# Dealing projection steps beside attention and mLSTM heads with a carried balance, and three more of them at the first head

## The chip, the cores and the metric

The kernel runs on one core of a Trainium2 chip. The metric is the time of one execution on the device in microseconds (us); the tables give a median over runs, and the profile shows one of these executions instruction by instruction. PE is TensorE (the matrix engine, PEld its weight loads), DVE is VectorE, ACT is ScalarE, POOL is GpSimd, SP issues most of the transfers.

## The reference

One layer of a hybrid decoder: 512 tokens, model width 2048, float32. Both branches read the same normed input through one projection `w_in`; their gated sums go through `w_out`.

```python
h = rms_norm(x, norm_g)
q_a, k_a, v_a, o_a, i_a, f_a, z_a, c_q, c_kv, k_r, z_b, g_a, g_b = split(h @ w_in)
# branch A: 8 mLSTM heads (qk 128, v 256)
q_a, k_a = split(silu(causal_depthwise_conv(concat(q_a, k_a), conv_w)))   # 4 taps
h_a = rms_norm(mlstm_chunkwise(q_a, k_a, v_a, i_a + b_i, f_a + b_f), mlstm_norm_g)
y_a = (sigmoid(o_a) * h_a * silu(z_a)) @ w_a
# branch B: latent attention, 16 heads (128 + 64 rotary)
q_b = rms_norm(rms_norm(c_q, q_lat_g) @ w_uq)      # then rope on the last 64
k_b, v_b = rms_norm(c_kv, kv_lat_g) @ w_ukv        # k_b normed with k_r, then rope
o_b = causal_softmax_attention(q_b, k_b, v_b)
y_b = (o_b * silu(z_b)) @ w_b
out = x + (sigmoid(g_a) * y_a + sigmoid(g_b) * y_b) @ w_out
```

## The kernel before

Every large product is made of three matmuls of a high and a low part of each operand (`mm3`, L113): ACT casts the high part, DVE subtracts for the low part (`split`, L104 to 107; its instructions show as L105 and L106). Weights stream in tiles through the SP queue and are split as they are used (`load_w`, L142). A projection is a generator that issues one step of its inner dimension at a time and yields how many columns PE was given: 6144 for a token-wise step with 512 columns (`proj_tok`, L169), 4608 with 384, 3072 for a channel-wise step of two blocks (`proj_ch`, L183).

The order of the work is written out by hand, and the framework then sorts each engine's queue by its own estimate of when an instruction can run. The parts are:

1. Latents, norm and the products of most of `w_in` in a seven-product (Strassen) form, to about 1040 us. Gates, values and the like go to DRAM and are read again later.
2. Latent transposes (two generators, four requests of 2000 each) beside the first of eight q/k blocks of `w_in` (`block_qk`, 16 steps of 3072); then the first pair projection; the mLSTM gates (requests of 6000, 3000 and 4000) beside the second block.
3. Attention in eight pairs of heads (`pair_attn`, L931). Each pair makes 11 requests for filler, the first of 8000 (`KEYS_AHEAD`), ten of 7800 (`ATTN_STEP`). In a request S is scores and softmax, X the transposes of the probabilities, O the product with the values. Beside pairs 0 to 6 the filler is the rest of a begun q/k block, then the projection of the next pair (`pair_proj`: four steps of 4608, four of 6144; behind it POOL takes a reciprocal root and scales the keys, L809 to 829), then further q/k blocks. What is left of a begun block and of the projection is drained at the end of each pair (L1076). Beside pair 7 the filler is the first seven steps of the `w_b` projection (`out_b`, L1044), a cap set by memory that opens only after attention.
4. mLSTM heads (`heads`, L1229): eight heads with eight requests each (`MLSTM_STEP`): four for the decay-weighted products j (`wda`, `wdb`, `sta`, `stb`), four for the sums i with the values (`num`). Within the same requests the convolution of the next head (`head_conv`), its loads (`head_load`) and the scaling and transposing of the previous head (`head_scale`, `head_out`) are issued. After the last head four requests (`OUT_AHEAD`) stand around its scaling. The filler is the rest of `w_b`, 64 steps of 6144 in all. Ahead of the heads the convolution and loads of head 0 are issued in turn with filler steps (L1251 to 1255).
5. What is left of `w_b` (L1259), then `w_a` and `w_out`. `w_a` reads the gated heads back from DRAM (`reload`, L1017; `ga_d`), at most six tiles ahead.

Requests meet filler in `weave` (L201): for each request it takes steps until the columns asked for are reached. A step can't be divided, and what a step gives beyond the request is forgotten with the next one.

Of the kernel before, what the change touches and what calls it, by code (L numbers as in the profile page):

```python
# [36 lines left out]
NB_RAW, NB_W, NB_L, NB_A, NB_B, NB_HEAD, NB_T, NB_ACC, NB_AUX = 4, 3, 2, 15, 12, 17, 6, 5, 3  # L37
NB_X, NB_RING, NB_HI, NB_LO = 5, 8, 3, 2

KEYS_AHEAD, ATTN_STEP, MLSTM_STEP, OUT_AHEAD, G_AHEAD = 8000, 7800, 4500, 8000, 6  # L40
EARLY = {"lat", "c", "gz", "vh", "vl", "rope", "rk"}


# [1 line left out]
def hybrid_kernel(  # L45
# [151 lines left out]
    def drain(gen):  # L197
        for _ in gen:
            pass

    def weave(main, filler):  # L201
        for want in main:
            while want > 0:
                got = next(filler, None)
                if got is None:
                    break
                want -= got


    sap = open_pool("sap")  # L210
# [833 lines left out]
    def out_b(d):  # L1044
        def evac(t, ps):
            u = u_t[d]
            V.scalar_tensor_tensor(u[:, t, :], u[:, t, :], 1.0, ps, ALU.add, ALU.mult)

        for k, want in enumerate(proj_tok(load_w(w_b, d * 512, 512, KD), 512, get_gb, KD, evac)):
            if k == H8:  # L1050
                u_t.append(pools["up"][1].tile([P, T, 512], F32, tag=f"u{d}", name=f"u{d}"))
                SP.dma_start(u_t[d], gb_g[d])
            yield want

    cs = [dict() for _ in range(8)]
    blocks = [block_qk(n) for n in range(8)]
    weave(chain(*lats), blocks[0])
    drain(blocks[0])
    drain(pair_proj(0, cs[0]))
    weave(mlstm_gates(), blocks[1])  # L1060
    drain(blocks[1])
    del blocks[:2]
# [9 lines left out]
    for p in range(7):  # L1072
        proj = pair_proj(p + 1, cs[p + 1])
        first = chain(ahead(True), proj)
        weave(pair_attn(p, cs[p]), chain(first, ahead()))
        drain(first)  # L1076
        cs[p] = None
# [8 lines left out]
    filler = chain(*(out_b(d) for d in range(4)))  # L1086
# [7 lines left out]
    def head_conv(h, c):  # L1094

        xs, parts = [], []
        for n in range(2):
            xp = tmp(516, "xp")
            G.memset(xp[:, 0:3], 0.0)
            SP.dma_start(xp[:, 3:515], qk_d[h][:, n, :])  # L1100
            xs.append(xp)

        def conv(n):
            xp, k = xs[n], 8 * n + h
            o = big([P, 2, S], F32R, "qkT")
            c["kT" if n else "qT"] = o
            b = tmp(512, "cv")

            def taps(j0, j1):
                for j in range(j0, j1):  # L1110
                    V.scalar_tensor_tensor(b, xp[:, j:j + S], cw[:, k, j:j + 1], b, ALU.mult, ALU.add)

            with behind_weights():
                V.tensor_scalar(b, xp[:, 3:515], cw[:, k, 3:4], None, ALU.mult)
                taps(0, 1)
            yield
            taps(1, 3)
            th = xp[:, 0:512]
            A.activation(th, b, AF.Tanh, scale=0.5)
            yield  # L1120
            V.scalar_tensor_tensor(b, th, 1.0, b, ALU.add, ALU.mult)
            A.copy(o[:, 0, :], b)
            yield
            V.tensor_tensor(o[:, 1, :], b, f32(o[:, 0, :]), ALU.subtract)
            yield

        q, k = conv(0), conv(1)
        for turn in ((), (), (), (q,), (q, k), (q, k), (q, k), (k,)):
            for part in turn:
                next(part)  # L1130
            yield
# [97 lines left out]
    def heads():  # L1229
        for h in range(H_A):  # L1230
            conv = ahead = iter(())
            if h + 1 < H_A:
                conv, ahead = head_conv(h + 1, hs[h + 1]), head_load(h + 1, hs[h + 1])
            for n, want in enumerate(head_mlstm(h, hs[h])):
                next(conv, None)
                next(ahead, None)
                if h and n == 4:
                    head_scale(h - 1, hs[h - 1])
                if h and n == 6:
                    head_out(h - 1, hs[h - 1])  # L1240
                yield want
            drain(conv)
            drain(ahead)
        for _ in range(2):
            yield OUT_AHEAD
        head_scale(H_A - 1, hs[H_A - 1])
        for _ in range(2):
            yield OUT_AHEAD
        head_out(H_A - 1, hs[H_A - 1])

    start = head_conv(0, hs[0])  # L1251
    for load in head_load(0, hs[0]):
        next(start)
        next(filler)
    drain(start)
    weave(heads(), filler)
    close_pool("bph")
    g2p = open_pool("g2p")
# [82 lines left out]
```

## Time and profile before

| | us |
|---|---|
| median of 3 runs | 2158.21 (2154.21 to 3683.05) |
| profiled execution, its own time | 2155.99 |
| its span, first to last instruction | 2154.3 |
| PE busy in it | 2101.4 (98%) |
| DVE busy | 1461.9 (68%) |
| ACT busy | 1007.7 (47%) |
| POOL busy | 167.4 (8%) |

A profile row gives what an engine did and, in brackets, how long it stood idle before it and what released it. PEclk is the clock that TensorE was granted, as a share of 2.4 GHz; it has two levels, 1.2 and 2.4 GHz, so a value between 0.5 and 1 is a mixture over the stretch. Matmuls are pipelined, so one that lasts 0.39 us on its row can be followed by the next after 0.23 us.

### The profile page before, as it was taken

To read this page: it belongs to the slowest core of one execution; us is meant where nothing else is said; L and a number is where in the kernel's file an instruction comes from. 1 tells how busy PE (TensorE), PEld (TensorE's weight loads), DVE (VectorE), ACT (ScalarE), POOL (GpSimd) and SP (SyncE) were. 2 spreads that over 40 slices of the span, in tenths; PEclk is the share of its full clock that TensorE was granted. 3 is DMA by queue.
4 is the path that set the end of the run, shared out by engine and by line. 5 is a ranking of instruction groups with operands and counts; after the bars stand their busy time and mean duration, and the time that the engine had idled before them with its cause. 6 is when DMAs were issued, how large, how long until landed. Compare 5 with 4: busy or idle time off the path is not lost. (4 is left out here: it accounts for less than half of the span.)

```text
span 2154.3 us, 30176 instructions
## 1 busy us (share of the span) xinstructions
PE 2101.4 (98%) x10776; PEld 1803.1 (84%) x10776; DVE 1461.9 (68%) x2304; ACT 1007.7 (47%) x2025; POOL 167.4 (8%) x306
## 2 busy tenths in 40 slices
PE   8999999999999999999999999989999978999999
PEld 8888888888888999988888888877778866888889
DVE  6888888887778778788556566568787764443233
ACT  8544455444444444444454455466455553222221
POOL 0000100000000000000022222033111110000000
PEclk9999999999999999999999999999999988999999
DMA  6655535633652452462733333432475536332443
GB/s 171 169 178 176 172 114 193 220 114 97 186 152 88 152 176 79 138 205 86 261 103 102 99 102 103 120 94 84 137 245 191 182 133 199 109 136 93 135 130 118
DMA packets 210183, 309.17 MB, mean 144 GB/s; under 512 B 31984, under 2 KB 99952, under 8 KB 209008
## 3 DMA queue, kind: packets, MB, share of 16 engines
q1 hardware_dynamic: 187248, 271.58, 41.0%
q10 hardware_dynamic: 22784, 35.66, 4.7%
q8 instruction: 84, 1.38, 0.3%
q14 instruction: 67, 0.55, 0.1%
HBM read 252.66 MB, written 54.53 MB: 143 GB/s over the span
## 5 line engine op out<-in xcount | busy, mean ns | idle before, releaser
L106 DVE TENSOR_TENSOR wlo<-raw,whi 128x512 fp32r<-128x512 f32 (+3 forms) x368 | 243.4, 663 | 327.1 <-PE acc L115 232.9
L105 ACT CAST whi<-raw 128x512 fp32r<-128x512 f32 (+3 forms) x368 | 218.9, 596 | 445.9 <-PE acc L116 322.7
L106 DVE TENSOR_TENSOR wl<-rx,wh 128x1024 fp32r<-128x1024 f32 x192 | 234.9, 1224 | 131.5 <-PE aux L535 58.8
L105 ACT CAST wh<-rx 128x1024 fp32r<-128x1024 f32 x192 | 202.4, 1055 | 211.3 <-PE acc L536 97.2
L105 ACT CAST wh<-rr 128x1024 fp32r<-128x1024 f32 x144 | 151.7, 1053 | 200.6 <-PE aux L536 91.7
L114 PE MATMUL acc<-whi,g 128*128 128x512 f32 x512 | 199.3, 397 | 8.1 <-ACT g L105 6.8
L115 PE MATMUL acc<-wlo,g 128*128 128x512 f32 x512 | 202.2, 395 | 0.3 <-DVE wlo L106 0.3
L116 PE MATMUL acc<-whi,g 128*128 128x512 f32 x512 | 201.9, 394 | 0.0
L106 DVE TENSOR_TENSOR wl<-rr,wh 128x1024 fp32r<-128x1024 f32 x144 | 175.7, 1220 | 31.5 <-PE aux L535 13.9
L535 PE MATMUL acc<-wl,sh 128*128 128x512 f32 x400 | 155.6, 389 | 0.0
L536 PE MATMUL acc<-wh,sl 128*128 128x512 f32 x400 | 155.6, 389 | 0.0
L534 PE MATMUL acc<-wh,sh 128*128 128x512 f32 x400 | 155.4, 389 | 0.0
L114 PEld LDWEIGHTS acc<-whi,g 128*128 128x128 f32 x512 | 96.3, 190 | 26.7 <-ACT g L105 7.2
L483 DVE TENSOR_TENSOR rx<-rr,rx 128x1024 f32<-128x1024 f32 x96 | 116.9, 1222 | 2.2
L115 PEld LDWEIGHTS acc<-wlo,g 128*128 128x128 f32 x512 | 97.3, 190 | 20.7 <-DVE wlo L106 2.0
L116 PEld LDWEIGHTS acc<-whi,g 128*128 128x128 f32 x512 | 97.1, 190 | 20.3 <-DVE g L106 0.2
L114 PE MATMUL acc<-whi,y 128*128 128x512 f32 (+1 forms) x320 | 111.1, 348 | 0.0
L116 PE MATMUL acc<-whi,y 128*128 128x512 f32 (+1 forms) x320 | 111.0, 347 | 0.0
L115 PE MATMUL acc<-wlo,y 128*128 128x512 f32 (+1 forms) x320 | 111.0, 347 | 0.0
L114 PE MATMUL acc<-whi,lat 128*128 128x384 f32 (+1 forms) x256 | 94.9, 373 | 0.8 <-ACT junk L792 0.5
L115 PE MATMUL acc<-wlo,lat 128*128 128x384 f32 (+1 forms) x256 | 93.5, 365 | 0.0
L534 PE MATMUL aux<-wh,sh 128*128 128x512 f32 x240 | 93.4, 389 | 0.0
(389 smaller groups left out, 5293.4 us busy)
## 6 DMA issues: line engine op xcount, KB each, us to landing
rr<-in_w_in SPq DMA_DIRECT2D x144, 512.0 KB, 4.6
rx<-in_w_in SPq DMA_DIRECT2D x48, 512.0 KB, 5.0
raw<-in_w_in SPq DMA_DIRECT2D x64, 256.0 KB, 2.8
raw<-in_w_b SPq DMA_DIRECT2D x64, 256.0 KB, 3.6
raw<-in_w_a SPq DMA_DIRECT2D x64, 256.0 KB, 3.1
raw<-in_w_out SPq DMA_DIRECT2D x64, 256.0 KB, 3.0
raw<-in_w_ukv SPq DMA_DIRECT2D x32, 256.0 KB, 2.9
raw<-in_w_uq SPq DMA_DIRECT2D x32, 192.0 KB, 2.4
```

The source lines that it names most:

```text
L105: hi = A.copy(dst_hi, src)
L106: lo = V.tensor_tensor(dst_lo, src, f32(dst_hi), ALU.subtract)
L114: PE.matmul(ps, lh, rh, start=start, stop=False)
L115: PE.matmul(ps, lh, rl, start=False, stop=False)
L116: PE.matmul(ps, ll, rh, start=False, stop=stop)
L483: V.tensor_tensor(dst, a, b, ALU.subtract)
L534: PE.matmul(out[i], lh[:, tok], hi[:, n, :], start=first, stop=False, skip_group_check=cont)
L535: PE.matmul(out[i], lh[:, tok], lo[:, n, :], start=False, stop=False, skip_group_check=cont)
L536: PE.matmul(out[i], ll[:, tok], hi[:, n, :], start=False, stop=k == H8 - 1, skip_group_check=cont)
```

## The change

`weave` carries a balance: each request is added to it, steps are taken while it is positive, and their columns come off it, so that a surplus counts against the next request. The balance starts at zero in each call. When the filler is used up, the rest of the main work is drained. Two constants are smaller, `MLSTM_STEP` 3900 instead of 4500 and `OUT_AHEAD` 6000 instead of 8000. At the first head, where the remaining two parts of its convolution were drained without filler, three turns issue one part (if any is left) and one filler step each.

```diff
--- before.py
+++ after.py
@@ -37,7 +37,7 @@
 NB_RAW, NB_W, NB_L, NB_A, NB_B, NB_HEAD, NB_T, NB_ACC, NB_AUX = 4, 3, 2, 15, 12, 17, 6, 5, 3
 NB_X, NB_RING, NB_HI, NB_LO = 5, 8, 3, 2
 
-KEYS_AHEAD, ATTN_STEP, MLSTM_STEP, OUT_AHEAD, G_AHEAD = 8000, 7800, 4500, 8000, 6
+KEYS_AHEAD, ATTN_STEP, MLSTM_STEP, OUT_AHEAD, G_AHEAD = 8000, 7800, 3900, 6000, 6
 EARLY = {"lat", "c", "gz", "vh", "vl", "rope", "rk"}
 
 
@@ -199,12 +199,15 @@
             pass
 
     def weave(main, filler):
+
+        balance = 0
         for want in main:
-            while want > 0:
+            balance += want
+            while balance > 0:
                 got = next(filler, None)
                 if got is None:
-                    break
-                want -= got
+                    return drain(main)
+                balance -= got
 
 
     sap = open_pool("sap")
@@ -1252,7 +1255,9 @@
     for load in head_load(0, hs[0]):
         next(start)
         next(filler)
-    drain(start)
+    for _ in range(3):
+        next(start, None)
+        next(filler)
     weave(heads(), filler)
     close_pool("bph")
     g2p = open_pool("g2p")
```

## Rows read from the trace of the kernel before

**Rows 1.** The first line of the page, the profiled execution

```profile
span 2154.3 us, 30176 instructions
```

**Rows 2.** Windows: stretch, length; busy PE, PEld, DVE, ACT, POOL; clock, DMA share, GB/s

```profile
150.00:200.00 50.00, 50.00 (x223) 41.39 (x222) 38.63 (x45) 23.35 (x26) 0.00 (x0) 1.00 0.68 201
...
1350.00:1400.00 50.00, 50.00 (x264) 42.99 (x263) 28.41 (x66) 23.09 (x51) 2.83 (x6) 1.00 0.42 125
1400.00:1450.00 50.00, 42.81 (x219) 36.45 (x218) 33.88 (x88) 32.85 (x108) 14.26 (x17) 0.93 0.31 95
1450.00:1500.00 50.00, 46.56 (x255) 38.85 (x254) 41.18 (x108) 32.91 (x113) 16.49 (x21) 1.00 0.27 87
1500.00:1550.00 50.00, 46.98 (x252) 38.22 (x252) 38.24 (x102) 25.94 (x66) 12.51 (x18) 1.00 0.23 80
1550.00:1600.00 50.00, 47.08 (x215) 38.22 (x214) 36.22 (x68) 22.78 (x56) 5.27 (x25) 0.97 0.84 284
...
1650.00:1700.00 50.00, 50.00 (x257) 42.55 (x255) 38.42 (x83) 27.30 (x73) 7.82 (x29) 1.00 0.58 190
...
1750.00:1800.00 50.00, 28.52 (x132) 23.73 (x131) 29.64 (x67) 25.41 (x65) 5.58 (x16) 0.73 0.44 147
1800.00:1850.00 50.00, 50.00 (x230) 41.31 (x229) 21.78 (x33) 14.66 (x25) 0.00 (x0) 1.00 0.48 159
```

**Rows 3.** Timeline of POOL and PE at pair 5: start, length, instruction, [idle before, releaser]

```profile
1423.78 2.93 POOL L121 TENSOR_TENSOR rs_y<-ms,mhalf 128x16 f32<-128x16 f32 x1 [11.38 <-DVE ms L811]
...
1431.26 1.11 PE L867 MATMUL aux<-ident,kn 128*128 128x128 f32 x4 [5.41 <-POOL kn L829]
```

**Rows 4.** Timeline of PE around the end of pair 6

```profile
1497.87 0.48 PE L114 MATMUL acc<-whi,g 128*128 128x512 f32 x1
...
1513.96 0.60 PE L867 MATMUL aux<-ident,qn 128*128 128x128 f32 x4
```

**Rows 5.** Timeline of PE in the heads: heads 2 and 6 begin, one filler step

```profile
1624.14 0.39 PE L1158 MATMUL aux<-nT,pick 128*128 128x512 f32 x1
...
1736.31 0.40 PE L114 MATMUL acc<-whi,g 128*128 128x512 f32 x1
...
1739.04 0.39 PE L1158 MATMUL aux<-nT,pick 128*128 128x512 f32 x1
```

**Rows 6.** Timeline of PE at the end of the heads, three longest waits

```profile
1759.82 0.80 PE L114 MATMUL aux<-qkT,qkT 128*128 128x512 f32 x1 [3.93 <-ACT qkT L1122]
...
1780.65 1.94 PE L1221 MATMUL aux<-ident,og 128*128 128x128 f32 x8 [4.84 <-DVE og L1215]
...
1789.36 0.79 PE L114 MATMUL acc<-whi,g 128*128 128x512 f32 x1 [6.77 <-ACT g L105]
```

**Rows 7.** Windows of 5 us with a granted clock below 1.00, columns as in rows 2

```profile
1430.00:1435.00 5.00, 3.74 (x16) 3.74 (x17) 1.71 (x3) 1.85 (x3) 2.48 (x4) 0.50 0.00 0
...
1580.00:1585.00 5.00, 5.00 (x19) 4.02 (x19) 5.00 (x10) 3.71 (x11) 0.00 (x0) 0.80 0.91 312
...
1760.00:1765.00 5.00, 2.53 (x7) 1.69 (x7) 2.31 (x8) 1.25 (x5) 2.21 (x7) 0.50 0.25 86
1765.00:1770.00 5.00, 2.88 (x10) 2.29 (x11) 4.29 (x11) 3.13 (x9) 1.31 (x3) 0.50 0.00 0
1770.00:1775.00 5.00, 5.00 (x31) 4.80 (x30) 0.58 (x2) 3.40 (x12) 0.07 (x1) 0.69 0.00 0
...
1790.00:1795.00 5.00, 5.00 (x16) 3.96 (x15) 4.24 (x8) 3.71 (x7) 0.00 (x0) 0.64 1.01 378
```

**Rows 8.** Timeline of DVE in head 1, head 2 and the last head

```profile
1619.99 0.69 DVE L106 TENSOR_TENSOR wlo<-raw,whi 128x512 fp32r<-128x512 f32 x1 [3.82 <-issue]
...
1626.37 0.69 DVE L1183 SCALAR_TENSOR_TENSOR wda<-aux,wda 128x512 f32<-128x512 f32 x1 [1.30 <-POOL vl L1141]
...
1763.75 0.48 DVE L1215 SCALAR_TENSOR_TENSOR og<-num,rsn,og 128x256 f32<-128x256 f32 x1 [2.65 <-POOL rsn L1208]
```

**Rows 9.** Timeline of the SP queue, transfers of the gated heads

```profile
1784.13 7.64 SPq L1023 DMA_DIRECT2D g<-ga  x13
```

## The prediction, made before the result was known

> **What bounds the kernel now.** I read the page first: the span [rows 1] and, in the 40 slices, a TensorE (PE) busy almost everywhere except in the slices around 1430 and around 1780 us. Then the table of windows of 50 us [rows 2]: the 25 windows from 150 to 1400 us (first and last shown) are a full 50.00 of PE, and so is the first one after 1800 us, where the two last projections begin. What PE idles behind its start-up lies in two places: 7.19 + 3.44 + 3.02 + 2.92 = 16.6 us in 1400 to 1600 (the last attention pairs and the first mLSTM head) and 21.5 us in 1750 to 1800 (the last heads). So PE's work is the bound, and this change neither adds nor removes a matmul. It can win only what PE waits, and what runs slowly because PE has waited.
>
> The second part is read from windows of 5 us [rows 7]. Where PE had just waited, the granted clock is 0.50, the lower of its two levels (1.2 against 2.4 GHz), or a mixture. The time lost is busy time times (1 - clock): 3.74 x 0.5 = 1.9 us at 1430, 5.00 x 0.2 = 1.0 at 1580, 1.3 + 1.4 + 1.6 at 1760 to 1775, 1.8 at 1790; together 9.0. Idle and slow time make a pool of 16.6 + 21.5 + 9.0 = 47.1 us. If all of it went, the span would be 2107.2.
>
> **Why PE waits there.** Every step of attention or a head asks for filler columns, and a `weave` without a balance rounds each request up to whole steps and forgets the surplus. I counted the steps by hand from the code.
>
> - Attention. 7800 columns are served as three q/k block steps (9216), or two projection steps (9216 to 12288). The six remaining blocks, 96 steps, are gone in the fourth request of pair 4; its last three requests and the last seven of pairs 5 and 6 get nothing. That leaves 13.7 us of idle time in 1400 to 1550 (16.6 less the 2.9 of the first head's window). The longest piece is a pair boundary [rows 3]: the reciprocal root on POOL begins at 1423.78, and PE's transposes of the scaled keys wait 5.41 us for POOL until 1431.26.
> - Heads. A request of 4500 is served by one whole step of 6144. 64 steps less 7 (pair 7) less 6 (head start) are 51, one for each request; they end with the third request of head 6. Five requests of head 6 and all eight of head 7 run bare, and nothing is left for the tail. The chain of PE's waits shows it [rows 6]: 3.93 us for the convolved q/k of head 7, 4.84 for the scaled output, 6.77 for the first reloaded gate rows, whose transfers were issued behind the last stores [rows 9].
>
> **The change, part by part.**
>
> 1. *Balance in attention.* The 11 requests of a pair are 86,000 columns; pair projection is 43,008 (4 x 4608 + 4 x 6144). With the surplus carried, a pair takes 28 block-sized steps instead of 33, so the blocks last into the fifth request of pair 6, and only its last request is empty. The gaps inside pairs 4, 5 and 6 should close. What stays: the balance is zeroed at each `weave`, and the projection now ends late. In pair 5 four block steps follow it, 24 matmuls of 2.73 / 12 = 0.228 us [rows 5], 5.5 us against the POOL chain of 1431.26 - 1423.78 = 7.5 [rows 3]: I take 1 us of wait with attention's own matmuls in between. In pair 6 no filler follows, so I put the whole old boundary there once more: 5.4 + 1.9 of slow clock. Pair 7 still has seven steps, now over five requests instead of four, as its cap is unchanged; the order of the queues already spreads them, as a w_b matmul at 1497.87, well ahead of pair 7's first transposes at 1513.96, shows [rows 4]. I leave it the 3.0 us of window 1500 to 1550. New waits: 1 + 7.3 + 3.0 = 11.3 us. Bounds: 0, if w_b steps are drawn into the boundary, and the 13.7 + 1.9 of now, if nothing closes.
>
> 2. *Three more steps at the first head.* They are 36 matmuls, 8.2 us at 2.73 a step [rows 5], with three weight loads, three splits on ACT and on DVE (0.69 us each on DVE [rows 8]), and splits of reloaded rows. They stand beside head 0's convolution, where PE waited 2.9 us and ran 1.0 us too slowly [rows 2, 7]. The splits come into DVE's queue ahead of head 0's own chain, where DVE is full (5.00 of 5 us at 1580 [rows 7]): about 2 us, under 8.2 us of PE. New wait 1 us; bounds 0 and 3.9.
>
> 3. *Balance in the heads, 3900 instead of 4500.* 48 steps are left. 64 requests of 3900 take 249,600 / 6144, rounded up 41; the four of 6000 at the end make it 45, and three are left for the drain. Head 0 gets 6, every other head 5, the tail 4 + 3. A head takes 28.73 us now, (1739.04 - 1624.14) / 4 from the first matmul of head 2 to that of head 6, eight steps of 2.73 in it [rows 5]. With five, PE needs 28.73 - 3 x 2.73 = 20.5 us. This is the doubtful step, as a head then has to fit DVE too. DVE is busy 38.42 of 50 us amid the heads, or 22.1 us in 28.73 [rows 2]; three splits less make 20.0. Its waits in the chain of a head come on top: 1.30 us for the exponentials and the causal selection before the first product [rows 8]; the 3.82 us wait there is slack and goes first. 20.0 + 1.3 = 21.3. The upper bound adds the 2.65 us that DVE stood behind POOL's reciprocal root in the bare head [rows 8]: 24.0. The lower is PE's 20.5. I take 22.0, in the middle, because a step now is either there or not (requests get 1, 0, 1 ...), so PE meets the bare chain three times a head: 1.5 us of idle time, 10 us over heads 1 to 7; bounds 0 and 7 x 3.5 = 24.
>
> 4. *Tail.* Two steps before the last scaling and two behind it, 10.9 us, cover the 4.84; the three drained, 8.2 us, cover the 6.77 [rows 5, 6]. The 13 gate transfers keep SP for 7.64 us [rows 9], and weight loads behind them may be late: 1 us; bounds 0 and 7.
>
> 5. The same `weave` beside the latents gives six steps instead of eight, beside the gates five as before; a drain follows each at once and PE is full there: nothing, as the same matmuls fill the same stretch. If they did not, it would cost at most the two steps that leave, 12 matmuls of 0.228 us or 2.7 us. `return drain(main)` does what the old `break` did.
>
> **Sum.** 2154.3 - 47.1 + 11.3 + 1 + 10 + 1 = 2130.5 us of span. The profiled run's time was 1.7 us above its span (2155.99), so 2132; the median of the shown runs, 2158.21, is 2.2 above the profiled run. That is 1.2% below the median, well inside the 2% (some 43 us) that a measurement of this kernel can tell from no change.
>
> **Rivals.**
>
> - *The clock sags.* Thin filler makes many short waits instead of a few long ones. For: at 1580 the clock averaged 0.80 [rows 7], though that window of 50 us held but 2.9 us of waits [rows 2]. Against: 1450 to 1550 has 6.5 us of short waits at 1.00 [rows 2]. With half of that sag, 0.90, over seven heads of 20.5 us: 144 x (1 / 0.9 - 1) = 16 us more, 2148. The Trainium skill ("TensorE: Matmul & The Clock Gate", section "A second HAM failure mode: psum-queue depth-cycling") says that frequent small idles between groups of matmuls make the clock go back and forth between its two levels; by that rule the heads would get slower exactly because filler is rationed. The trace agrees with it at 1580 and disagrees at 1450 to 1550, so it gets a small chance.
> - *The heads become a chain, and the kernel gets slower.* DVE takes its queue in order; if the scaling of the previous head is put ahead of a head's first product, as in the bare head at 1763.75 [rows 8], each head stands behind POOL's reciprocal root and the convolution behind that. Without the heads' idle time the gain is 47.1 - 13.3 = 33.8 us, or 4.8 us for each of seven heads: from a period of 25.3 us on, the kernel is slower than before. If the period stayed at 28.7, it would be 7 x 8.2 = 57 us of idle time, 2154.3 - 33.8 + 57 = 2178 of span, 2180. Against: DVE's 22.1 us contain no such wait now. Slower by 2% needs a period above 31.
> - *Dealing changes nothing.* The order on the queues is not the written one [rows 4]; if that order already moves filler to where it is needed, only names change: 2152 to 2160. Against: rows 6 show waits that no order could fill, since no step was left.
> - *Nearly all waits go.* No boundary stall and heads at PE's 20.5: 2109 to 2115.
>
> **How the numbers follow.** Forecast (2116 to 2146) 0.68; clock 0.10; heads slower than before 0.08; nothing 0.07; nearly all 0.07. The predicted time is the forecast's 2132. The range runs from 2112, half way into the last case, to 2151, past the clock case; that leaves out some 0.18. Faster by over 2% needs under 4 us of new waits in all: 0.05. Slower by over 2%: 0.02. Within 2%: 0.93.
>
> **What would show it.** Right: no window from 1440 to 1500 with more than 1 us idle; one wait of about 5 us for the scaled keys before pair 7 and none before pair 5; first matmuls of heads 20.5 to 23.5 us apart; nothing above 2 us between the last head and the first w_a matmul; a clock of 1.00 in the heads. Wrong: heads 25 us or more apart, with PE waiting for products or convolutions of DVE; a clock below 0.9 in several windows of the heads; w_a's first weights late.

## The result, and the profile after

| | before | changed |
|---|---|---|
| median, us | 2157.07 (4 runs) | 2136.43 (2135.75 to 2137.48, 4 runs) |
| ratio to the kernel before | | 0.9909, 95% interval 0.9890 to 0.9929 |
| span of the profiled execution | 2154.3 | 2135.0 |

The change saves 20 us, 0.9%; 2132 had been predicted, in a range of 2112 to 2151. The single outlying run of the kernel before (3683.05) is left out of the ratio.

Windows of 50 us of the changed kernel answer to [rows 2], with the same columns:

```profile
1350.00:1400.00 50.00, 49.36 (x266) 42.92 (x265) 34.70 (x84) 27.88 (x88) 14.19 (x18) 1.00 0.33 98
1400.00:1450.00 50.00, 45.94 (x237) 40.09 (x236) 28.83 (x74) 25.61 (x82) 12.76 (x14) 0.97 0.35 103
1450.00:1500.00 50.00, 47.16 (x238) 39.78 (x237) 36.77 (x87) 29.35 (x78) 6.52 (x8) 0.96 0.41 136
1500.00:1550.00 50.00, 44.28 (x228) 37.01 (x225) 31.95 (x84) 25.11 (x69) 10.03 (x16) 0.93 0.23 80
1550.00:1600.00 50.00, 47.97 (x226) 39.79 (x225) 39.17 (x72) 22.46 (x51) 3.33 (x15) 0.97 0.81 280
...
1650.00:1700.00 50.00, 47.63 (x254) 40.46 (x255) 44.57 (x97) 32.15 (x90) 10.65 (x33) 1.00 0.63 206
...
1750.00:1800.00 50.00, 48.14 (x217) 39.62 (x216) 26.42 (x42) 21.67 (x36) 1.39 (x6) 1.00 0.69 236
1800.00:1850.00 50.00, 50.00 (x230) 41.29 (x229) 19.23 (x29) 12.72 (x22) 0.00 (x0) 1.00 0.33 114
```

PE's idle time in 1750 to 1800 has gone from 21.5 us to 1.9. In its place every window of the heads has a little (2.4 us in 1650 to 1700, where there was none). But in 1400 to 1550 there are 4.1 + 2.8 + 5.7 = 12.6 us, where there were 13.7, and 0.6 in 1350 to 1400, where there was none: beside attention the idle time has only moved.

Where PE stands now is in its timeline (start, length, instruction, idle before it and releaser); the lines answer to [rows 3, 5, 6]:

```profile
1434.23 0.39 PE L116 MATMUL acc<-whi,lat 128*128 128x512 f32 x1
...
1447.19 1.11 PE L870 MATMUL aux<-ident,kn 128*128 128x128 f32 x4 [4.06 <-POOL kn L832]
...
1485.55 0.44 PE L910 MATMUL aux<-ident,pr 128*128 128x128 f32 x2 [1.26 <-DVE go L931]
...
1490.25 0.52 PE L910 MATMUL aux<-ident,pr 128*128 128x128 f32 x3 [1.31 <-ACT junk L795]
...
1515.21 1.12 PE L870 MATMUL aux<-ident,kn 128*128 128x128 f32 x4 [5.65 <-POOL kn L832]
...
1568.80 1.43 PE L114 MATMUL acc<-whi,g 128*128 128x512 f32 x4 [1.80 <-ACT whi L105]
...
1598.30 0.39 PE L1161 MATMUL aux<-nT,pick 128*128 128x512 f32 x1
...
1707.62 0.39 PE L1161 MATMUL aux<-nT,pick 128*128 128x512 f32 x1
...
1760.83 1.03 PE L1224 MATMUL aux<-ident,og 128*128 128x128 f32 x8
...
1771.90 0.50 PE L114 MATMUL acc<-whi,g 128*128 128x512 f32 x1 [1.86 <-ACT g L105]
```

Two pair boundaries wait for the scaled keys, 4.06 us ahead of pair 6 and 5.65 ahead of pair 7; before the change it was one of 5.41. In pair 6 there are two waits of 1.3 us, released by DVE's gated output (`go`) and by ACT's sums of squares (`junk`). The start of the first head waits 1.80 us. From the first matmul of head 1 (1598.30) to that of head 6 (1707.62) it is 21.9 us a head. The transposes of the last head at 1760.83 wait for nothing, and the first matmul of `w_a`, at 1771.90, waits 1.86 us instead of 6.77.

Windows of 5 us of the changed kernel, to be set beside [rows 7]:

```profile
1445.00:1450.00 5.00, 2.81 (x11) 2.61 (x12) 0.84 (x2) 1.27 (x2) 3.18 (x4) 0.67 0.14 45
...
1485.00:1490.00 5.00, 3.26 (x13) 2.11 (x13) 4.80 (x14) 4.77 (x15) 0.00 (x0) 1.00 0.65 220
1490.00:1495.00 5.00, 4.65 (x14) 3.63 (x15) 5.00 (x10) 4.60 (x20) 4.38 (x4) 0.66 0.38 113
...
1515.00:1520.00 5.00, 4.79 (x23) 4.43 (x24) 2.23 (x4) 3.17 (x6) 1.80 (x4) 0.66 0.01 2
...
1570.00:1575.00 5.00, 4.77 (x16) 3.67 (x16) 3.10 (x6) 2.88 (x7) 0.29 (x1) 0.70 0.68 247
```

The clock still falls behind four of these waits, to 0.66 to 0.70 as a mean of 5 us, but not behind the 1.86 us ahead of `w_a`; busy time times (1 - clock) is 0.9 + 1.6 + 1.6 + 1.4 us. In the heads it stays at 1.00.

The gain by place: the last stores of attention's outputs are issued 1.3 us later than before. The SP queue before and after:

```profile
1552.13 0.33 SPq L929 DMA_DIRECT2D gb<-go  x1
...
1553.44 0.32 SPq L932 DMA_DIRECT2D gb<-go  x1
```

From there to the first `w_a` matmul it is 1789.36 - 1771.90 + 1.3 = 18.8 us less, and the 1.8 us of slow clock behind it are gone [rows 6, 7]. So the heads bring all of the 19.3 us of span, and attention brings nothing.

### The profile page after: what moved, and what is told of

It is laid out like the page before. It is cut to its first block, busy times and chain, and to the rows that moved or that the text cites. A ratio compares the mean times of both kernels' runs of the same rounds, so it can differ in the third digit from the quotient of the medians.

```text
span 2135.0 us, 30145 instructions
## 1 busy us (share of the span) xinstructions
PE 2096.4 (98%) x10776; PEld 1801.6 (84%) x10776; DVE 1458.9 (68%) x2304; ACT 1005.9 (47%) x2025; POOL 173.0 (8%) x306
## 5 line engine op out<-in xcount | busy, mean ns | idle before, releaser
L116 PEld LDWEIGHTS acc<-whi,g 128*128 128x128 f32 x512 | 96.6, 189 | 20.1
L114 PE MATMUL acc<-whi,lat 128*128 128x384 f32 (+1 forms) x256 | 94.7, 372 | 0.2
L116 PE MATMUL acc<-whi,lat 128*128 128x384 f32 (+1 forms) x256 | 93.4, 365 | 0.0
```

The lines of the kernel that those rows point to most:

```text
L114: PE.matmul(ps, lh, rh, start=start, stop=False)
L116: PE.matmul(ps, ll, rh, start=False, stop=stop)
```

## Which place the gain comes from

First the balance beside attention alone, with the heads dealt as before:

```diff
     def weave(main, filler):          # with the balance, as changed
+    def weave_whole(main, filler):    # the old loop, whole steps
...
-    weave(heads(), filler)
+    weave_whole(heads(), filler)
-... MLSTM_STEP, OUT_AHEAD ... = ... 3900, 6000
+... MLSTM_STEP, OUT_AHEAD ... = ... 4500, 8000
-    for _ in range(3):                # three steps at the first head
-        next(start, None)
-        next(filler)
+    drain(start)
```

> The balance is kept beside the latents, gates and attention; the heads are dealt as before (whole steps, 4500 and 8000, no three extra steps). Theory: the whole gain is in the heads, and the balance only moves attention's waits from pairs 5 and 6 to two pair boundaries; in the changed kernel the last product of attention ended at 1552.5 us against 1551.2 before. Expected 2155 to 2160, no faster than before. Rival, the prediction's first term (the gaps of pairs 4 to 6 close, one boundary stays): 4 us less than before, about 2152. Rival, attention carries a good part of the 20 us: 2147 or less.

Measured: 2158.83 us, ratio 1.0005 (0.9995 to 1.0014). The balance beside attention alone brings nothing, neither the 4 us of the prediction nor more.

Then the other half:

```diff
-    weave(chain(*lats), blocks[0])
+    weave_whole(chain(*lats), blocks[0])       # and so beside gates and all pairs
     weave(heads(), filler)                     # balance, 3900, 6000 and three steps stay
```

> The balance works in the heads alone; attention is dealt as before, with 3900, 6000 and the three extra steps kept. Theory: 2133 to 2137, the same as the changed kernel or 1 to 3 us better, since the balance beside attention brought nothing. Rival, attention's balance is worth 4 us: 2140. Rival, worth much more: 2145 or above.

Measured: 2134.17 us, ratio 0.9889 (0.9875 to 0.9904), at least as good as the whole change. The gain is that of the heads, with their start and their tail.

What the balance beside attention costs shows at the first head. PE's longest wait there is 0.60 us in this kernel, at a clock of 1.00, against 1.80 us and 0.70 in the changed one; with the heads dealt as before the change, it is 2.74 us with the balance beside attention and 1.11 without:

```profile
1572.31 0.50 PE L115 MATMUL acc<-wlo,g 128*128 128x512 f32 x1 [0.60 <-DVE wlo L106]
```

## The three steps at the first head

```diff
-    for _ in range(3):
-        next(start, None)
-        next(filler)
+    drain(start)
```

> The changed kernel without the three steps at the first head: the end of head 0's convolution is drained bare, and six steps are left behind the heads instead of three. The prediction gave these steps 2.9 us (3.9 us of waits and slow clock less 1). In the changed kernel PE still waited 1.8 us there for the cast of a weight whose ACT queue stood behind the convolution, and the clock read 0.70 for 5 us, so some 3.5 us were not won. Theory: 2136 to 2138, 0 to 2 us worse than the changed kernel, as the steps come back in the drain. Rival: 2139 or more, if they really cover head 0's chain.

Measured: 2142.89 us, ratio 0.9929 (0.9914 to 0.9944), against 0.9909 and 0.9913 for the changed kernel: some 4 us worse, though the intervals overlap and the two did not run side by side. My expectation of 0 to 2 fell, and the rival, which was the prediction's own term, holds. Windows of 5 us of this kernel at the first head:

```profile
1570.00:1575.00 5.00, 2.65 (x11) 2.00 (x12) 4.79 (x10) 3.75 (x10) 0.51 (x1) 1.00 0.98 379
...
1580.00:1585.00 5.00, 3.67 (x24) 3.00 (x22) 4.81 (x12) 1.69 (x5) 0.61 (x3) 1.00 1.08 360
1585.00:1590.00 5.00, 3.85 (x11) 3.09 (x12) 5.00 (x8) 3.58 (x13) 0.00 (x0) 0.66 0.79 269
```

PE idles 2.4, 1.3 and 1.2 us in them and the clock falls, while DVE is 4.8 to 5.0 of 5 us busy. The longest wait is released by ACT, whose queue stands behind DVE's convolution of head 1:

```profile
1584.83 0.63 ACT L1122 ACTIVATE xp<-cv 128x512 f32<-128x512 f32 x1 [2.82 <-DVE cv L1114]
...
1586.15 0.58 PE L114 MATMUL aux<-vh,sta 128*128 128x258 f32 x1 [2.49 <-ACT junk L1199]
```

So head 0's products and head 1's convolution share DVE, and PE has too little to do beside them. The three steps cover most of that: PE's idle time in 1550 to 1600 is 5.0 us without them and 2.0 in the changed kernel, where the one long wait left is that of 1.80 us.

## What sets the pair boundary

POOL takes the reciprocal root of queries and keys together (16 columns: one power and four small steps), then scales the queries' root and the rotary keys, then the keys, for which PE waits. An experiment orders the keys first:

```diff
-        rsqrt(rs[all 16], ms[all 16], 16)
-        srq = ...; (rotary queries); krs = ...
-        G.tensor_tensor(kn, kn, rs[keys], ALU.mult)
+        rsqrt(rs[keys], ms[keys], 8)
+        G.tensor_tensor(kn, kn, rs[keys], ALU.mult)
+        rsqrt(rs[queries], ms[queries], 8)
+        srq = ...; (rotary queries); krs = ...
```

> The changed kernel with another order of POOL's work behind each pair projection: the reciprocal root of the keys alone (8 columns instead of 16) and the scaling of the keys come first, the queries' root and the rotary keys after. The chain that PE waits for at a pair boundary gets shorter by about 1.3 us for the root, 1.3 us for what stood before the scaling and, with 0.2 more, to some 4.5 us from 7.5. Theory (the two boundary waits of 4.1 and 5.7 us are this chain and nothing else): each shrinks by some 3 us, 2130 to 2133 in all. Rival, something else releases PE there (convolved or rotary operands, weights): the waits move to the next instruction, 2135 to 2137.

Measured: 2133.69 us, ratio 0.9891 (0.9875 to 0.9908). The waits are 3.2 and 5.1 us, shorter by 0.8 and 0.6 only. POOL's timeline ahead of pair 7 shows why:

```profile
1503.41 3.27 POOL L121 TENSOR_TENSOR rs_y<-ms,mhalf 128x8 f32<-128x8 f32 x2 [12.31 <-DVE ms L814]
...
1507.92 1.89 POOL L817 TENSOR_TENSOR kn<-kn,rs 128x1024 f32<-128x1024 f32 x1
```

Both roots (x2) stand ahead of the scaling: the framework's sort had put the queries' root up, so the chain from POOL's start to the scaled keys was 6.4 us instead of 7.4. The time is just above the theory's 2130 to 2133. The second version holds it back:

```diff
+        scaled = G.tensor_tensor(kn, kn, rs[keys], ALU.mult)
+        with tc.issue_after(scaled.ins):
+            rsqrt(rs[queries], ms[queries], 8)
```

> The changed kernel with the keys' root and scaling first on POOL, and the queries' root held in POOL's queue until the scaling is issued. The run before, without the hold, had both roots side by side ahead of the scaling: the chain from POOL's start to the keys' transposes fell only from 7.4 to 6.4 us, and each boundary wait by 0.6 to 0.8. Now the chain should be 1.7 (root of 8 columns) + 0.9 + 1.9 = 4.5 us. Theory (POOL's chain and nothing else): boundary waits of about 1 and 2.7 us instead of 4.1 and 5.7, 2128 to 2132. Rival (the next operand is late as well): waits move on, 2133 or more.

Measured: 2130.71 us, ratio 0.9886 (0.9871 to 0.9900). The timeline of PE at the two boundaries:

```profile
1441.88 0.66 PE L872 MATMUL aux<-ident,kn 128*128 128x128 f32 x4 [1.09 <-POOL kn L817]
...
1444.93 0.66 PE L858 MATMUL aux<-ident,krs 128*128 128x128 f32 x4 [1.26 <-POOL krs L834]
...
1507.26 0.90 PE L872 MATMUL aux<-ident,kn 128*128 128x128 f32 x4 [3.44 <-POOL kn L817]
```

The waits for the keys fall to 1.09 and 3.44 us, about as expected, and 1.26 us (0.85 at pair 7) come back behind them for the rotary keys, now behind the queries' root on POOL. So POOL's chain does release these waits. The shorter one is worth some 6 us beside the changed kernel on the same chip (2137.19 us, ratio 0.9913, next section); the 4 us of the first version rest on ratios whose intervals overlap, from kernels that did not run side by side.

But POOL's 7.4 to 7.8 us are only the second half of what has to be covered. In the changed kernel the last matmul of pair 6's projection is at 1434.23 and the keys' transposes run at 1447.19: 13 us. ACT and DVE first evacuate the projection, and POOL begins at 1439.4:

```profile
1439.39 2.93 POOL L121 TENSOR_TENSOR rs_y<-ms,mhalf 128x16 f32<-128x16 f32 x1 [12.20 <-DVE ms L814]
```

Attention's own matmuls fill some 2.7 us of the 13, so by this count seven or eight steps of 1.37 us have to lie behind the projection. The deal of the changed kernel has eight or more behind those of pairs 0 to 3, then six, four and none behind pairs 4 to 6, and the waits were 0, 0, 0, 0, 0.6, 4.1 and 5.7 us.

## A deal by whole blocks

Six blocks are left for seven pairs. This version puts one whole block behind each of the first six projections, and requests enough for both:

```diff
-        first = chain(ahead(True), proj)
-        weave(pair_attn(p, cs[p]), chain(first, ahead()))
+        first = chain(proj, blocks.pop(0) if blocks else ())
+        weave(pair_attn(p, cs[p]), first)
-... ATTN_STEP ... = ... 7800
+... ATTN_STEP ... = ... 8400
```

With it ran the changed kernel itself, for a comparison on one chip:

> The changed kernel once more, on the chip of this group, so that the other three can be compared with it and not only with the kernel before. Expected 0.991 of the kernel before, about 2137, with PE waiting 4.1 and 5.7 us for the scaled keys at the two last pair boundaries.

Measured: 2137.19 us, ratio 0.9913 (0.9896 to 0.9929), with the boundary waits that the first profile had (4.06 and 5.63 us). In pair 6 it differs: one wait above 1 us (1.32) instead of two, and the clock stays at 1.00. Its windows there:

```profile
1485.00:1490.00 5.00, 3.46 (x15) 2.08 (x14) 4.79 (x14) 5.00 (x18) 1.35 (x2) 1.00 0.84 259
1490.00:1495.00 5.00, 4.58 (x19) 3.11 (x17) 5.00 (x10) 4.59 (x18) 3.45 (x3) 1.00 0.05 20
```

> The changed kernel with another deal in attention: beside each of pairs 0 to 5 the next pair's projection comes first and exactly one whole q/k block (16 steps) behind it, with requests of 8400 (92,000 columns a pair against 92,160 of filler); pair 6 has the projection alone. Theory: a pair boundary waits for POOL when fewer than about six block steps lie behind the projection (in the changed kernel 6 steps gave 0.6 us of wait, 4 gave 4.1, none 5.7, eight and more none); with 16 steps there is no wait, and the bare pair 6 has its projection done long before its end. Attention's idle time falls from some 15 us to some 6 and its slow clock goes: 2124 to 2130. Rival: the bare pair costs as much as the boundaries did: 2134 or more.

Measured: 2118.28 us, ratio 0.9825 (0.9810 to 0.9840), 19 us less than the changed kernel beside it and better than the theory's 2124. Its windows of 50 us:

```profile
1350.00:1400.00 50.00, 50.00 (x257) 42.67 (x257) 31.73 (x81) 26.50 (x87) 13.07 (x15) 1.00 0.34 101
1400.00:1450.00 50.00, 50.00 (x261) 43.19 (x260) 34.37 (x88) 27.27 (x88) 14.59 (x18) 1.00 0.30 87
1450.00:1500.00 50.00, 48.02 (x260) 40.15 (x260) 41.01 (x101) 34.00 (x102) 14.58 (x18) 1.00 0.45 153
1500.00:1550.00 50.00, 48.08 (x243) 38.67 (x241) 37.89 (x89) 24.20 (x54) 2.23 (x11) 1.00 0.51 178
```

No pair boundary waits for POOL. Attention idles 2.0 us in 1400 to 1550, all of it in short waits, and 1.9 more belong to the first head; the clock is 1.00 throughout. The first head begins at 1546.5 us instead of 1565.6 in the changed kernel's run of this group. Of the 19.1 us between, 13.0 are idle time (6.0 against 19.1 us from 24 us to the first head), 3.5 are slow clock behind the long waits, and the remaining 2.6 were not taken apart.

At the first head the two waits of this kernel add up to more than the 1.80 and 0.23 us of the changed one, and the clock stays at 1.00:

```profile
1548.64 1.19 PE L114 MATMUL acc<-whi,g 128*128 128x512 f32 x4 [1.74 <-ACT whi L105]
1550.36 0.50 PE L115 MATMUL acc<-wlo,g 128*128 128x512 f32 x1 [0.53 <-DVE wlo L106]
```

Does that add up with the heads? The same deal with the heads of the kernel before:

```diff
-    weave(heads(), filler)
+    weave_whole(heads(), filler)     # 4500, 8000, drain(start), as before the change
```

> One whole q/k block behind each projection beside pairs 0 to 5 (requests of 8400, balance kept there), but the heads dealt as before the change: whole steps, 4500 and 8000, no three extra steps. It asks whether attention's and the heads' gains add up. Theory: attention's waits and the heads' lie in different stretches, so this deal is worth here what it was worth on the changed kernel (19 us): 2135 to 2140. Rival, what is won in attention is lost again where filler runs out in the heads: 2146 or more.

Measured: 2138.84 us, ratio 0.9906 (0.9888 to 0.9925). PE's waits at the end of its heads are those of [rows 6] to a hundredth:

```profile
1742.45 0.80 PE L114 MATMUL aux<-qkT,qkT 128*128 128x512 f32 x1 [3.93 <-ACT qkT L1133]
...
1763.11 1.30 PE L1232 MATMUL aux<-ident,og 128*128 128x128 f32 x5 [4.85 <-DVE og L1226]
...
1771.81 0.80 PE L114 MATMUL acc<-whi,g 128*128 128x512 f32 x1 [6.76 <-ACT g L105]
```

The two gains add up within the noise: 0.9906 x 0.9909 = 0.9816, where 0.9825 (0.9810 to 0.9840) was measured for both. Last, both cures of the boundary in one kernel:

> The two changes that gained on the changed kernel in one: one whole block behind each projection, and the keys' root and scaling first on POOL with the queries' root held behind them. Theory: they cure the same wait, and with 16 block steps behind the projection no wait for the scaled keys is left, so the second adds nothing: 2115 to 2120, as with the first alone. Rival, POOL's chain still costs something within the pairs: 2112 or less.

Measured: 2117.43 us, ratio 0.9803 (0.9788 to 0.9818). The interval just meets that of the deal alone, the spans of the two profiled executions stand the other way (2116.1 against 2113.2), and no wait for the scaled keys is left in either. Whether POOL's order adds anything there stays open.

## What limits a head

```diff
-... MLSTM_STEP ... = ... 3900
+... MLSTM_STEP ... = ... 3200
```

> The changed kernel with requests of 3200 instead of 3900 in the heads: four steps a head instead of five, ten left for the drain instead of three. It asks what else than PE limits a head. PE alone would need 28.73 - 3.9 x 2.73 = 18.1 us a head. Theory (DVE and the chain limit it): DVE needs 19.15 us a head in the changed kernel, 18.4 with one split less, and 1 to 2 us of waits on top: heads 20 to 21 us apart, PE idle 2 to 3 us in each instead of 0.7, 2144 to 2152. Rival (PE limits a head even so): heads 18 to 18.5 us apart, and the same total, 2135 to 2139.

Measured: 2145.20 us, ratio 0.9948 (0.9934 to 0.9963). From head 1 to head 6, and the stretch between:

```profile
1594.69 0.39 PE L1161 MATMUL aux<-nT,pick 128*128 128x512 f32 x1
...
1695.41 0.40 PE L1161 MATMUL aux<-nT,pick 128*128 128x512 f32 x1
```

```profile
1594.70:1695.40 100.70, 93.21 (x496) 78.39 (x495) 88.51 (x195) 65.59 (x178) 22.51 (x75) 0.98 0.64 208
```

A head takes 20.1 us in the mean of five, 2 more than the estimate from PE's matmuls. PE idles 1.5 us in each, less than the 2 to 3 expected, and its clock is 0.98; DVE is busy 17.7 us. In the changed kernel the same stretch (109.3 us) is

```profile
1598.30:1707.60 109.30, 105.15 (x556) 88.80 (x555) 93.17 (x203) 67.95 (x185) 25.49 (x76) 1.00 0.61 197
```

with 0.8 us of idle time a head and DVE busy 18.6 of 21.9 (the expectation had 19.15). So one step less takes 2.7 us of matmuls out of a head and shortens it by 1.7, and the kernel is 8 us slower. The longest waits with four steps are released by DVE, 1.24 us for `wda` and 1.88 for `wlo`:

```profile
1654.20 0.80 PE L115 MATMUL acc<-wlo,g 128*128 128x512 f32 x1 [1.88 <-DVE wlo L106]
```

Behind the latter the clock falls once, to 0.74:

```profile
1655.00:1660.00 5.00, 5.00 (x17) 3.99 (x17) 3.36 (x12) 2.65 (x8) 1.03 (x3) 0.74 0.39 132
```

What limits a head at four steps is thus PE's own work, 18.6 us of 20.1, plus waits for DVE's chain. Whether 20 us is a floor was not tried with still fewer steps.

The other way:

```diff
-... MLSTM_STEP ... = ... 3900
+... MLSTM_STEP ... = ... 4500
```

> The changed kernel with the old request of 4500 in the heads, balance kept: 47 of the 48 steps go into the heads (six each, five in the last), one stands in the tail and none is left for the drain. It asks what the smaller constant is for. Theory: heads 28.73 - 2.1 x 2.73 = 23 us apart with less PE idle time in each, but at the end the waits for the scaled output and for the first reloaded rows come back (4.8 and 6.8 us before, with one step of 2.7 us against them, and slow clock behind them): 2141 to 2148. Rival, the balance alone is what counts: 2135 to 2139.

Measured: 2148.23 us, ratio 0.9944 (0.9928 to 0.9959). At its end:

```profile
1771.59 1.82 PE L1224 MATMUL aux<-ident,og 128*128 128x128 f32 x8 [4.33 <-DVE og L1218]
...
1780.53 0.80 PE L114 MATMUL acc<-whi,g 128*128 128x512 f32 x1 [7.12 <-ACT g L105]
```

The two waits of the tail are back, 4.33 and 7.12 us, since only one step is left to lie in them; heads 1 to 5 begin 24.2 us apart. So 3900 is no detail: with the old request the rest of the change brings 12 of the 20 us.

## Why the prediction was right, and where it was not

- *The bound and the pool.* PE's idle and slow time, 47.1 us in two places, was the right frame: nearly all that these kernels won came out of it. The shortest span, 2113.2, is 6 us above the floor of 2107.2. The pool was 2 us too small: the windows of 5 us at 1575 (0.86), at 1425 (0.84) and from 1780 to 1790 (0.50) had a slow clock too and were not added.
- *Heads.* Predicted were 22.0 us a head, 10 us of idle time over seven of them and 1 us in the tail. Measured: 21.9 us, some 5 us over the seven (0.8 us a head from head 1 to head 6), 1.9 us in the tail. The path was right: PE is the bound and DVE with its waits comes close behind. That 22.0 and 21.9 agree so well is partly luck, as the terms behind it were off both ways: PE was taken at 20.5 us a head and is busy 21.0, its idle time at 1.5 and is 0.8, DVE at 20.0 and is busy 18.6. The rival in which each head stands behind POOL's root and the convolution did not come: DVE was busy in 18.6 of 21.9 us.
- *First head.* 2.9 us were predicted for the three steps; without them the kernel is some 4 us slower. The step holds, though 2.0 us of idle time and 1.4 of slow clock stayed where I had left 1.
- *Attention.* This step failed. I gave it 4.3 us (15.6 of now against 11.3 of new waits); it brought nothing. The mis-sized term is the boundary ahead of pair 6: 1 us predicted, 4.06 and 0.9 of slow clock measured. I had set four block steps against POOL's 7.5 us [rows 3], from the start of POOL's root, and left out the five us in which ACT and DVE evacuate the projection; from its last matmul it is 13 us. Ahead of pair 7, where the old boundary was put whole, 5.4 + 1.9 became 5.65 + 1.6, while the 3.0 us left for the short waits of 1500 to 1550 nearly vanished: the boundary accounts for all but 0.1 of that window's idle time. The first sign of being right also failed, since 2.2 us are idle in 1445 to 1450 and 1.7 in 1485 to 1490.
- *A wait not foreseen.* In pair 6, PE waits 1.26 and 1.31 us and then runs at 0.66. The second execution of the same kernel has a single wait above 1 us there and no slow clock, though nearly as much idle time in 1450 to 1500 (2.7 us against 2.8). In the first, ACT is busy 4.77 and DVE 4.80 of 5 us. Of the casts of the reloaded value outputs for `w_b`, ten lay between 1394 and 1438 before the change, and thirteen now fall between 1475 and 1496: the blocks last longer, so the memory that those rows need comes free later, and they arrive in a burst. This cause is read from the order of the queues and was not tried by itself.
- *The sum.* 2132 against 2136.4 is closer than its terms. Idle and slow time left beside attention was put at 11.3 us and came to some 19; at the first head 1 became 3.5, in the tail 1 became 1.9. Some 5 us less of idle time in the heads and the 2 us that the pool lacked made up for over half of it, which is luck.
- *The clock.* Nothing of the clock rival was seen in the heads of the changed kernel, 1.00 with waits of up to 1 us; with requests of 3200 it fell once. The Trainium skill ("TensorE: Matmul & The Clock Gate", section "A second HAM failure mode: psum-queue depth-cycling") tells of a kernel in which frequent small idles between groups of matmuls made the clock go back and forth; by that rule rationed heads should have lost time, and at 3900 they did not. At the first head it fell to 0.70 behind waits of 1.80 and 0.23 us, and in pair 6 behind two of 1.3. But in the deal by whole blocks it stayed at 1.00 behind 1.74 and 0.53 us. So in these traces waits of one to two us do not settle by their length whether the clock falls.

## What to carry to other kernels

Filler is a budget: count its steps by hand against all requests, with the rounding, and see where the last one falls. A step that follows what the next stage needs is worth more than one ahead of it, so deal the work that has a long chain behind it first and cover that chain, from its last matmul to its first reader, with what nobody waits for. The Trainium skill ("Perfetto Trace Analysis", section "Optimization Strategy") says that interleaving stretches with different bounds may help; these runs agree, 20 us in the heads and 19 us in attention. They add that too little filler costs time as well: with four steps a head instead of five PE's waits nearly doubled, from 0.8 to 1.5 us a head, and the kernel lost 8 us.

## What the runs showed of the hardware

POOL's power instruction, which makes the reciprocal root, lasts 2.93 us for 128 x 16 elements and 1.67 for 128 x 8, while a multiplication of 128 x 8 takes 0.20: here the power for a tiny root costs about as much as scaling 128 x 1024 keys (1.90). POOL's timeline in the kernel with the held root:

```profile
1437.05 1.67 POOL L121 TENSOR_TENSOR rs_y<-ms,mhalf 128x8 f32<-128x8 f32 x1 [12.11 <-DVE ms L814]
1438.79 0.20 POOL L122 TENSOR_TENSOR rs_t<-ms,rs_y 128x8 f32<-128x8 f32 x1
...
1439.93 1.90 POOL L817 TENSOR_TENSOR kn<-kn,rs 128x1024 f32<-128x1024 f32 x1
```

TensorE's granted clock can differ between two executions of one kernel at the same place: in pair 6 of the changed kernel it was 0.66 in one and 1.00 in the other, with 4.65 and 4.58 of 5 us busy.
